# PSUM banks of an encoder layer's front shared out anew, and low-rank weights filled up to 128 rows

## The chip, the cores and the metric

The kernel runs on one core of one Trainium2 chip. TensorE (PE) multiplies 128-row tiles into PSUM, which has eight banks of 128 partitions x 512 float32; VectorE (DVE), ScalarE (ACT) and GpSimd (POOL) read the banks and compute elementwise; SyncE (SP) issues transfers, and ACT issues some as well. Each engine works through its own queue in order and waits on semaphores. The metric is the device time of one launch in microseconds, the median over runs.

## What is computed

One layer of an encoder on 256 tokens of width 1024: an input projection, two token mixers on its columns (a gated linear recurrence `hgrn2` with 8 heads of 128, and an RWKV-7 recurrence with 16 heads of 64, both in both directions), a gated merge of their outputs, a layer norm, and a mixture of 32 experts of which each token takes four. The part that the change touches is the RWKV branch's low-rank projections (`wl` and `a_lo` are 64 columns wide each):

```python
r, k, v, wl_f, wl_b, a_lo, g_lo = _split(p, RW_SPLITS)
decays = []
for d, wl in enumerate((wl_f, wl_b)):
    w = -jax.nn.softplus(-(w0[d] + jnp.tanh(wl) @ w_up[d])) - 0.5
    decays.append(jnp.exp(-jnp.exp(w)))
a = jax.nn.sigmoid(a0 + a_lo @ a_up)
g = jax.nn.sigmoid(g_lo) @ g_up
```

## The kernel before, in words

The **front** takes the tokens, transposes them (L188) and forms all products with the input weights. `dense_parts` (L129) is one dense product: it takes a PSUM bank `bank_d` (`bd`), loads two tiles of weights of 512 KB on SP's queue, and multiplies sixteen times (L154), 128 rows by 128 columns by 256 tokens. Readers on ACT, DVE or POOL then empty the bank. All small per-column parameters are loaded by fifteen transfers on ACT's queue into one tile `prm` (L182), which PE transposes once (L195) into a bank `bank_p`.

The RWKV branch works on four quarters `qi` of its columns (four heads each). For each, `rwkv_columns` makes the dense products, `rwkv_prepare` (L417) prepares the chunked form of the recurrence, and `rwkv_run` (L622) runs it, with banks `bank_c` (two) and `bank_y` (one). In `rwkv_prepare` the function `pair(r)`, called twice, multiplies the low-rank activations `lora` with `wup` (one product for each direction, L472) and with `aup` (L479), forms the bonus (L491, read by DVE at L492), and then the products of decayed keys (L546, 16 program matmuls for each direction, masked by DVE at L553). All of these take a bank `bank_p` (`bs`), of which there is one. `wup` holds the two directions one below the other, 64 rows each, so each product has a contraction of 64 rows. Then `inverse` inverts the 16 x 16 triangles on DVE by repeated steps (L581, L583) and joins them with small products (L598, L607), also in `bank_p`. `hgrn_mix` (L778) does the other mixer with one bank `bank_h`: DVE makes `KK` (L784), PE multiplies with it (L810, L811, then groups at L827, each copied out by DVE at L829), and the gate `og` reads a dense product's bank on ACT (L774) and DVE (L775).

The streams of work are generators that `interleave` (L377) merges by rates; the Tile scheduler then orders each engine's queue by a model of its own, in which the number of banks of each kind counts. So a change of the banks changes the order of many instructions. Once `rwkv_run` has finished, the **merge** follows (L1010 and on), and then the **experts**: their weights, 402 MB, stream through rings of SBUF tiles, and PE multiplies each as it lands (L1202, L1232). The order in that half is written out by hand.

The eight banks are shared out at L98.

Of the kernel before, what the change touches and what calls it, by code (L numbers as in the profile page):

```python
# [8 lines left out]
F32 = mybir.dt.float32  # L9
# [7 lines left out]
P = 128  # L17
S = 256
# [30 lines left out]
def tile_encoder(ctx: ExitStack, tc: tile.TileContext, A, out):  # L49
    nc = tc.nc  # L50
    V, SC, G, T = nc.vector, nc.scalar, nc.gpsimd, nc.tensor
# [40 lines left out]
    fc = front.enter_context(tc.tile_pool(name="fc", bufs=1))  # L92

    def bank(tag, bufs=None):
        return ps.tile([P, 512], F32, name="bank_" + tag, tag=tag, bufs=bufs)


    bd, bs, bc, bh, by = (lambda t=t, n=n: bank(t, n) for t, n in (("d", 3), ("p", 1), ("c", 2), ("h", 1), ("y", 1)))  # L98

    def cp(eng, out, in_):  # L100
        if eng is SC:
# [71 lines left out]
    n = 0  # L173
# [10 lines left out]
    for k in range(0, KT, 2):  # L184
        b = bd()
        for kk in range(2):
            for t in range(2):
                T.transpose(out=b[:, kk * 256 + t * P:kk * 256 + (t + 1) * P],  # L188
                            in_=x_tok[:, t, (k + kk) * P:(k + kk + 1) * P], identity=ident)
# [4 lines left out]
    b = bs()  # L194
# [123 lines left out]


    lora = fc.tile([P, 3, S], F32, name="lora")  # L320
    b = lora1
    shift(lora[:, 0, :], b[:, :S], "muw")
    shift(lora[:64, 1, :], b[:64, S:], "mua", n=64)
    SC.activation(lora[:, 0, :], lora[:, 0, :], AF.Tanh)
    b = lora2
# [91 lines left out]
    def rwkv_prepare(qi, rw, tmp):  # L417
# [6 lines left out]
        vt = rw.tile([P, 2, 2, P], F32, name="vt", bufs=2)  # L424
        box[f"prep{qi}"] = L, Y, vt, bon, BS, scl
        cq = slice(256 * qi, 256 * qi + 256)
        wup = tmp.tile([P, 256], F32, name="wup")
        nc.scalar.dma_start(out=wup, in_=A["rw_w_up"][0].rearrange("a l n -> (a l) n")[:, cq])
        aup = tmp.tile([64, 256], F32, name="aup")
        nc.scalar.dma_start(out=aup, in_=A["rw_a_up"][0][:, cq])  # L430
        KB = late.tile([P, 2, 2, S], F32, name="KB", tag="B")


# [6 lines left out]
        b = bs()  # L440
        for r in range(2):
            for t in range(2):
                T.matmul(b[:, 4 * r + 2 * t:4 * r + 2 * t + 2], lhsT=sq[:, r, t * P:(t + 1) * P],
                         rhs=blk[:, 0:P:64], start=True, stop=True)
        rs = rsqrt(tmp, b[:, :8], 8, 1.0, 1e-24, floor=True)
        yield 2
        b = bs()
        for r in range(2):
            for t in range(2):
                for h in range(2):  # L450
                    n = 4 * r + 2 * t + h
                    T.matmul(b[64 * h:64 * h + 64, r * S + t * P:r * S + (t + 1) * P],
                             lhsT=rs[:, n:n + 1].to_broadcast([P, 64]), rhs=ident, start=True, stop=True)
# [11 lines left out]
        def pair(r):  # L465
# [3 lines left out]
            sg = tmp.tile([P, 2, S], F32, name="sg", tag="sg")  # L469
            b = bs()  # L470
            for d in range(2):
                T.matmul(b[:, d * S:(d + 1) * S], lhsT=wup[64 * d:64 * d + 64, cj],  # L472
                         rhs=lora[64 * d:64 * d + 64, 0, :], start=True, stop=True)
                SC.activation(sg[:, d, :], b[:, d * S:(d + 1) * S], AF.Tanh, scale=0.5,
                              bias=col(hm, "w0", 8 * d + j))
            V.tensor_scalar(sg, sg, 0.5, 0.5, op0=OP.mult, op1=OP.add)
            at = tmp.tile([P, S], F32, name="at")
            b = bs()
            T.matmul(b[:, :S], lhsT=aup[:, cj], rhs=lora[:64, 1, :], start=True, stop=True)  # L479
            sigmoid(at, b[:, :S], col(hm, "a0", j))  # L480
            yield 1
            V.scalar_tensor_tensor(out=KBr[:, 1, :], in0=ASr[:, 0, :], scalar=-1.0, in1=at,
# [516 lines left out]
    b = by()  # L999
# [485 lines left out]
```

## Time and profile before

| what | value |
| --- | --- |
| time, median of 3 runs | 1590.78 us (1585.95 to 1590.83) |
| the profiled execution, its own time | 1591.12 us |
| span of the profiled execution | 1589.3 us |
| mean granted TensorE clock | 0.981 |
| PE busy | 1455.9 us (92%) |
| DVE busy | 591.2 us (37%) |
| ACT busy | 374.4 us (24%) |
| POOL busy | 95.0 us (6%) |
| read from HBM | 464.48 MB, 293 GB/s over the span |

The span runs from the first to the last instruction; the 1.8 us between it and the execution's time lie outside of what the engines do. The shares of busy time are means over stages with different limits, so they are read stage by stage.

### The profile page before, as it was taken

How to read it: one execution, taken by the hardware profiler on the slowest of the kernel's cores; microseconds unless marked ns; L12 is line 12 of the kernel's file. 1: busy time of each engine (PE TensorE's matmuls, PEld its weight loads, DVE VectorE, ACT ScalarE, POOL GpSimd, SP SyncE). 2: the span in 40 equal slices, each digit the busy share in tenths (PEclk: the TensorE clock that was granted, in tenths of full speed). 3: DMA queues.
4: the chain of work that ended last, by engine and by line, in shares of the span. 5: the costliest groups of instructions: out<-in, count | busy, mean ns of one | idle time of the engine just before them, and what ended most of it. 6: DMA issues, size and time to landing. Idle time of an engine off the chain costs nothing. (4 is left out here: it accounts for less than half of the span.)

```text
span 1589.3 us, 27117 instructions
## 1 busy us (share of the span) xinstructions
PE 1455.9 (92%) x11331; PEld 796.7 (50%) x11331; DVE 591.2 (37%) x1539; ACT 374.4 (24%) x983; POOL 95.0 (6%) x142
## 2 busy tenths in 40 slices
PE   8989989989988999999999999889999988988985
PEld 7667667667666897444444433244434323322321
DVE  4685885985983465112111111121112111111113
ACT  2426335335335243211111111101111100100100
POOL 0310210210210000000000000000000000000000
PEclk9999999999999999999999999989899999999998
DMA  6322322322344786799999999999999999999995
GB/s 190 108 69 68 86 72 67 86 74 70 99 140 134 262 311 241 305 419 415 418 417 416 417 418 416 417 418 416 416 418 418 415 418 417 416 417 418 416 419 208
DMA packets 133981, 467.36 MB, mean 294 GB/s; under 512 B 9544, under 2 KB 66780, under 8 KB 101084
## 3 DMA queue, kind: packets, MB, share of 16 engines
q1 hardware_dynamic: 129280, 460.88, 74.5%
q10 hardware_dynamic: 4572, 4.68, 0.9%
q8 instruction: 91, 1.49, 0.4%
q14 instruction: 38, 0.31, 0.1%
HBM read 464.48 MB, written 1.05 MB: 293 GB/s over the span
## 5 line engine op out<-in xcount | busy, mean ns | idle before, releaser
L154 PE MATMUL bank_d<-xT,wt 128*128 128x256 f32 x1200 | 311.5, 398 | 0.4 <-DMA wt<-in_w_in_dram 0.4
L154 PEld LDWEIGHTS bank_d<-xT,wt 128*128 128x128 f32 x1200 | 217.4, 193 | 39.8 <-issue 6.2
L1238 DVE SCALAR_TENSOR_TENSOR yl<-ypb,slotg,yh 128x512 fp32r<-128x512 f32 x32 | 24.0, 751 | 483.2 <-ACT yh L1237 460.1
L1202 PE MATMUL hpb<-ring_l,xg 128*64 128x512 f32 x416 | 98.7, 602 | 4.7 <-DMA ring_l<-in_moe_w_dram 4.7
L1202 PE MATMUL hpb<-ring_p,xg 128*64 128x512 f32 x416 | 98.5, 598 | 2.4 <-DMA ring_p<-in_moe_w_dram 2.4
L1184 DVE TENSOR_SCALAR ot<-tpb 128x256 fp32r<-128x256 f32 x32 | 13.6, 425 | 233.9 <-ACT tpb L1183 233.9
L1202 PE MATMUL hpb<-ring_r,xg 128*64 128x512 f32 x408 | 96.3, 598 | 4.4 <-DMA ring_r<-in_moe_w_dram 4.4
L1237 ACT ACTIVATE yh<-ypb,slotg 128x512 fp32r<-128x512 f32 x32 | 22.0, 689 | 309.1 <-PE ypb L1232 309.1
L1163 PE MATMUL tpb<-oh,x 128*128 128x256 f32 (+1 forms) x288 | 65.1, 369 | 4.2 <-ACT xg L1168 3.2
L1183 ACT ACTIVATE tpb<-tpb 128x256 f32<-128x256 f32 x32 | 11.8, 370 | 235.3 <-PE tpb L1181 232.1
L1163 PEld LDWEIGHTS tpb<-oh,x 128*128 128x128 f32 x288 | 48.0, 190 | 35.6 <-DVE glu L1214 17.9
L1149 POOL TENSOR_TENSOR ohg<-oh,gate 128x512 f32<-128x512 f32 (+1 forms) x9 | 8.6, 952 | 867.6 <-PE tpb L1181 849.8
L1202 PEld LDWEIGHTS hpb<-ring_l,xg 128*64 128x64 f32 x416 | 29.0, 138 | 56.7 <-issue 40.6
L1202 PEld LDWEIGHTS hpb<-ring_r,xg 128*64 128x64 f32 x408 | 28.1, 136 | 54.7 <-issue 40.2
L1202 PEld LDWEIGHTS hpb<-ring_p,xg 128*64 128x64 f32 x416 | 27.8, 136 | 51.8 <-issue 42.5
L1232 PE MATMUL ypb<-ring_l,aT 128*64 128x512 f32 x208 | 48.8, 597 | 5.0 <-DMA ring_l<-in_moe_w_dram 5.0
L1232 PE MATMUL ypb<-ring_r,aT 128*64 128x512 f32 x200 | 47.3, 598 | 6.4 <-DMA ring_r<-in_moe_w_dram 6.4
L1202 PE MATMUL hpb<-ring_q,xg 128*64 128x512 f32 x200 | 47.2, 597 | 4.5 <-DMA ring_q<-in_moe_w_dram 4.5
L1232 PE MATMUL ypb<-ring_p,aT 128*64 128x512 f32 x192 | 45.0, 599 | 6.9 <-DMA ring_p<-in_moe_w_dram 6.9
L1202 PE MATMUL hpb<-ring_s,xg 128*64 128x512 f32 x208 | 49.2, 598 | 2.2 <-DMA ring_s<-in_moe_w_dram 2.2
L1216 ACT ACTIVATE sgm<-glu 128x256 f32<-128x256 f32 x64 | 26.7, 418 | 102.6 <-DVE glu L1214 102.6
L1202 PE MATMUL hpb<-ring_e,xg 128*64 128x512 f32 x208 | 48.6, 598 | 1.5 <-DMA ring_e<-in_moe_w_dram 1.5
(332 smaller groups left out, 2214.5 us busy)
## 6 DMA issues: line engine op xcount, KB each, us to landing
ring_l<-in_moe_w_dram SPq DMA_DIRECT2D x78, 1024.0 KB
ring_p<-in_moe_w_dram SPq DMA_DIRECT2D x76, 1024.0 KB
ring_r<-in_moe_w_dram SPq DMA_DIRECT2D x76, 1024.0 KB
wt<-in_w_in_dram SPq DMA_DIRECT2D x84, 512.0 KB
ring_s<-in_moe_w_dram SPq DMA_DIRECT2D x40, 1024.0 KB
ring_e<-in_moe_w_dram SPq DMA_DIRECT2D x38, 1024.0 KB
ring_q<-in_moe_w_dram SPq DMA_DIRECT2D x38, 1024.0 KB
ring_b<-in_moe_w_dram SPq DMA_DIRECT2D x38, 1024.0 KB
```

The source lines that it names most:

```text
L154: T.matmul(o, lhsT=lhsT, rhs=rhs, start=n == 0, stop=n == last)
L1149: G.tensor_tensor(out=ohg[:, :, :n], in0=oh[:, :, :n], in1=gate[:, :, es[0]:es[0] + n].unsqueeze(3).to_broadcast([P, 2, n, 64]), op=OP.mult)
L1163: T.matmul(b[:, kk * 256:kk * 256 + ne * 64], lhsT=x1[t][:, n * P:(n + 1) * P], rhs=oh[:, t, :ne].rearrange("p e s -> p (e s)"), start=t = ...
L1183: SC.activation(b[:, :S], b[:, :S], AF.Copy, accum_out=sg)
L1184: V.tensor_scalar(ot, b[:, :S], 0.0, None, op0=OP.is_gt)
L1202: T.matmul(self.hbs[cc][64 * j:64 * j + 64, :], lhsT=self.xg[:, k, self.ei, :], rhs=self.w1[k][:, c0:c0 + 512], start=False, stop=k == KT - 1)
L1216: SC.activation(sgm[cc], glu[cc], AF.Sigmoid, scale=1.702)
L1232: T.matmul(yb[64 * j:64 * j + 64, :], lhsT=self.aT[:, k % 4, 64 * (k // 4):64 * (k // 4) + 64], rhs=self.w2[k][:, j * 512:(j + 1) * 512], ...
L1237: SC.activation(yh, yb, AF.Copy, scale=self.sg)
L1238: V.scalar_tensor_tensor(out=yl, in0=yb, scalar=self.sg, in1=yh.bitcast(F32), op0=OP.mult, op1=OP.subtract)
```

## The change

One bank goes from the dense products to the preparations: `bank_d` has two in place of three, `bank_p` two in place of one. And the low-rank weights get a tile `ups` that lives through the whole front and has 128 rows for each of three products, the half that doesn't belong to the product being zero: direction 0 in rows 0 to 63, direction 1 in rows 64 to 127, `a` in rows 0 to 63. The zeros are written once at the start, by DVE, and so is the unused half of `lora`'s second part. Every quarter loads its columns into the other halves with three transfers on ACT's queue in place of two. The three products then have a contraction of 128 rows.

```diff
--- before.py
+++ after.py
@@ -95,7 +95,7 @@
         return ps.tile([P, 512], F32, name="bank_" + tag, tag=tag, bufs=bufs)
 
 
-    bd, bs, bc, bh, by = (lambda t=t, n=n: bank(t, n) for t, n in (("d", 3), ("p", 1), ("c", 2), ("h", 1), ("y", 1)))
+    bd, bs, bc, bh, by = (lambda t=t, n=n: bank(t, n) for t, n in (("d", 2), ("p", 2), ("c", 2), ("h", 1), ("y", 1)))
 
     def cp(eng, out, in_):
         if eng is SC:
@@ -318,6 +318,10 @@
 
 
     lora = fc.tile([P, 3, S], F32, name="lora")
+    V.memset(lora[64:128, 1, :], 0.0)
+    ups = fc.tile([P, 3, 256], F32, name="ups")
+    V.memset(ups[64:128, 0:3:2, :], 0.0)
+    V.memset(ups[0:64, 1, :], 0.0)
     b = lora1
     shift(lora[:, 0, :], b[:, :S], "muw")
     shift(lora[:64, 1, :], b[:64, S:], "mua", n=64)
@@ -424,10 +428,9 @@
         vt = rw.tile([P, 2, 2, P], F32, name="vt", bufs=2)
         box[f"prep{qi}"] = L, Y, vt, bon, BS, scl
         cq = slice(256 * qi, 256 * qi + 256)
-        wup = tmp.tile([P, 256], F32, name="wup")
-        nc.scalar.dma_start(out=wup, in_=A["rw_w_up"][0].rearrange("a l n -> (a l) n")[:, cq])
-        aup = tmp.tile([64, 256], F32, name="aup")
-        nc.scalar.dma_start(out=aup, in_=A["rw_a_up"][0][:, cq])
+        for d in range(2):
+            nc.scalar.dma_start(out=ups[64 * d:64 * d + 64, d], in_=A["rw_w_up"][0][d][:, cq])
+        nc.scalar.dma_start(out=ups[0:64, 2], in_=A["rw_a_up"][0][:, cq])
         KB = late.tile([P, 2, 2, S], F32, name="KB", tag="B")
 
 
@@ -469,14 +472,13 @@
             sg = tmp.tile([P, 2, S], F32, name="sg", tag="sg")
             b = bs()
             for d in range(2):
-                T.matmul(b[:, d * S:(d + 1) * S], lhsT=wup[64 * d:64 * d + 64, cj],
-                         rhs=lora[64 * d:64 * d + 64, 0, :], start=True, stop=True)
+                T.matmul(b[:, d * S:(d + 1) * S], lhsT=ups[:, d, cj], rhs=lora[:, 0, :], start=True, stop=True)
                 SC.activation(sg[:, d, :], b[:, d * S:(d + 1) * S], AF.Tanh, scale=0.5,
                               bias=col(hm, "w0", 8 * d + j))
             V.tensor_scalar(sg, sg, 0.5, 0.5, op0=OP.mult, op1=OP.add)
             at = tmp.tile([P, S], F32, name="at")
             b = bs()
-            T.matmul(b[:, :S], lhsT=aup[:, cj], rhs=lora[:64, 1, :], start=True, stop=True)
+            T.matmul(b[:, :S], lhsT=ups[:, 2, cj], rhs=lora[:, 1, :], start=True, stop=True)
             sigmoid(at, b[:, :S], col(hm, "a0", j))
             yield 1
             V.scalar_tensor_tensor(out=KBr[:, 1, :], in0=ASr[:, 0, :], scalar=-1.0, in1=at,
```

Lines behind the change stand two or three higher in the kernel after (L472 becomes L475, L479 L481, L546 L548, L598 L600, L784 L786, L810 L812, L827 L829).

The order of PE's queue at its start, before: L188 transposes the input tokens, L195 the parameters, L154 is a dense product's matmul.

```order
L188 MATMUL bank_d<-ident,x_tok 128x128 x16
L154 MATMUL bank_d<-xT_75,wt 128x256 x24
L195 MATMUL bank_p<-ident,prm 128x116
L154 MATMUL bank_d<-xT_75,wt 128x256 x40
L443 MATMUL bank_p<-blk,sq 128x2 x4
```

The same place after the change:

```order
L188 MATMUL bank_d<-ident,x_tok 128x128 x12
L195 MATMUL bank_p<-ident,prm 128x116
L188 MATMUL bank_d<-ident,x_tok 128x128 x4
L154 MATMUL bank_d<-xT_75,wt 128x256 x64
L446 MATMUL bank_p<-blk,sq 128x2 x4
L154 MATMUL bank_d<-xT_75,wt 128x256 x5
```

L195 has moved ahead of all dense matmuls, and to before the last four transpositions of the input.

PE's queue in the second half of the pair stretch of the third quarter, before (L472 and L479 are the low-rank products, L491 the bonus, L546 the decay products, L737 and L741 belong to the end of the recurrence of the quarter ahead), up to the products with `KK` at L810:

```order
L154 MATMUL bank_d<-xT_75,wt 128x256 x10
L491 MATMUL bank_p<-sqb,blk 128x256
L154 MATMUL bank_d<-xT_75,wt 128x256 x3
L546 MATMUL bank_p<-L,BK 64x64 x16
L154 MATMUL bank_d<-xT_75,wt 128x256 x4
L546 MATMUL bank_p<-L,BK 64x64 x16
L154 MATMUL bank_d<-xT_75,wt 128x256 x2
L737 MATMUL bank_c<-ident,yn 128x128
L741 MATMUL bank_c<-lora,gup 128x256
L154 MATMUL bank_d<-wt,xT_75 128x256 x8
```

The same place after, where L812 is the first product with `KK`:

```order
L154 MATMUL bank_d<-xT_75,wt 128x256 x2
L646 MATMUL bank_y<-W,L 32x64 x4
L154 MATMUL bank_d<-xT_75,wt 128x256 x7
L493 MATMUL bank_p<-sqb,blk 128x256
L154 MATMUL bank_d<-xT_75,wt 128x256 x2
L548 MATMUL bank_p<-L,BK 64x64
L154 MATMUL bank_d<-xT_75,wt 128x256 x2
L548 MATMUL bank_p<-L,BK 64x64 x31
L646 MATMUL bank_y<-W,L 32x64 x4
L154 MATMUL bank_d<-xT_75,wt 128x256 x18
L154 MATMUL bank_d<-wt,xT_75 128x256 x9
L812 MATMUL bank_h<-hq,KK 32x32
```

Dense matmuls have left the places between the preparation's products, and 27 of them stand in one block behind the last of L548, directly ahead of L812.

DVE's queue around `KK` of that quarter, before (L581 and L583 are the steps of the inverse, L743 and L745 the recurrence's end):

```order
L581 TENSOR_TENSOR R<-N 128x44
L745 SCALAR_TENSOR_TENSOR obT<-bon,pv,bank_c 128x256
L583 TENSOR_TENSOR N<-N,R 128x11x4
L743 SCALAR_TENSOR_TENSOR bon<-bank_c,pv,bon 128x256
L581 TENSOR_TENSOR R<-N 128x50
L784 TENSOR_SCALAR KK<-FT 128x2x512
L583 TENSOR_TENSOR N<-N,R 128x10x5
L745 SCALAR_TENSOR_TENSOR obT<-bon,pv,bank_c 128x256
```

And after, where L583 and L585 are these steps and L87 belongs to the root for the norm of the recurrence's output:

```order
L583 TENSOR_TENSOR R<-N 128x44
L86 SCALAR_TENSOR_TENSOR nw_t<-nw_t,nw_y 128x8
L785 TENSOR_TENSOR QQ<-FT,hq 128x1024
L585 TENSOR_TENSOR N<-N,R 128x4x11
L87 SCALAR_TENSOR_TENSOR nw_y<-nw_t,nw_y 128x8
L786 TENSOR_SCALAR KK<-FT 128x2x512
L583 TENSOR_TENSOR R<-N 128x36
L733 TENSOR_SCALAR yn<-bank_y,gn_mv,nw_y 128x64
```

`KK` has moved from behind the fifth step of its kind (L581) to behind the eleventh (L583), with the norm's root and its statistics between.

## Rows read from the trace of the kernel before

**Rows 1.** The page, part 2: busy tenths in 40 slices of the span.
```profile
DMA  6322322322344786799999999999999999999995
```

**Rows 2.** Windows: length, busy PE PEld DVE ACT POOL, clock, DMA share, GB/s.
```profile
500.00:560.00 60.00, 60.00 (x511) 50.90 (x512) 21.76 (x70) 16.70 (x38) 0.29 (x1) 1.00 0.66 222
700.00:900.00 200.00, 198.89 (x1022) 81.06 (x1018) 32.78 (x78) 26.68 (x60) 2.10 (x2) 1.00 1.02 417
```

**Rows 3.** Windows of one middle quarter: pair stretch, rest, inverse stretch.
```profile
274.60:311.00 36.40, 33.91 (x340) 24.04 (x339) 30.79 (x79) 13.93 (x39) 10.97 (x12) 1.00 0.29 79
221.70:274.60 52.90, 51.35 (x899) 38.84 (x899) 32.12 (x99) 28.02 (x98) 5.76 (x11) 0.95 0.22 62
193.90:221.70 27.80, 22.15 (x270) 17.33 (x266) 27.18 (x69) 8.55 (x19) 2.99 (x4) 0.98 0.35 101
```

**Rows 4.** Windows: first quarter's three stretches; the last's inverse and rest.
```profile
45.20:82.50 37.30, 34.87 (x255) 25.96 (x254) 26.91 (x49) 17.67 (x47) 13.96 (x12) 1.00 0.37 104
82.50:112.80 30.30, 24.72 (x359) 19.00 (x355) 28.02 (x72) 9.13 (x30) 3.47 (x5) 0.94 0.30 87
112.80:157.60 44.80, 43.64 (x781) 32.68 (x781) 26.15 (x83) 24.02 (x78) 3.51 (x8) 0.96 0.22 61
426.20:460.20 34.00, 27.60 (x295) 21.39 (x294) 30.24 (x75) 12.22 (x24) 2.96 (x4) 0.90 0.52 167
460.20:549.50 89.30, 82.23 (x1119) 65.04 (x1119) 40.55 (x124) 33.98 (x103) 6.48 (x11) 1.00 0.50 163
```

**Rows 5.** Timeline of the start: start, us, engine, line, tile; SP, ACT, PE.
```profile
0.76 0.86 SPq L164 DMA_DIRECT2D x_tok<-in_x_dram  x2
9.74 0.28 ACTq L182 DMA_DIRECT2D prm<-in_ln_b_dram  x1
4.57 0.45 PE L188 MATMUL bank_d<-ident,x_tok 128*128 128x128 f32 x1 [4.57 <-DVE smask L218]
6.05 3.17 PE L188 MATMUL bank_d<-ident,x_tok 128*128 128x128 f32 x15 [1.04 <-DMA x_tok<-in_x_dram]
9.06 10.54 PE L154 MATMUL bank_d<-xT,wt 128*128 128x256 f32 x48
20.12 1.10 PE L154 MATMUL bank_d<-xT,wt 128*128 128x256 f32 x4 [0.42 <-DMA wt<-in_w_in_dram]
```

**Rows 6.** Timeline of PE beside a pair of the preparation.
```profile
293.88 0.70 PE L472 MATMUL bank_p<-lora,wup 64*128 64x256 f32 x2
295.57 0.70 PE L472 MATMUL bank_p<-lora,wup 64*128 64x256 f32 x2
309.85 1.15 PE L546 MATMUL bank_p<-L,BK 64*64 64x64 f32 x32 [1.62 <-DVE L L553]
313.13 3.62 PE L154 MATMUL bank_d<-wt,xT 128*128 128x256 f32 x16
```

**Rows 7.** Groups by form: count | busy, mean ns | idle before, who ended it.
```profile
L546 PE MATMUL bank_p<-L,BK 64*64 64x64 f32 x512 | 19.3, 221 | 8.7 <-DVE L L553 5.1 <-DVE bon L492 3.2 <-DVE L L533 0.3
```

**Rows 8.** Timeline: last readers of a dense bank (ACT, DVE).
```profile
334.43 0.60 ACT L774 ACTIVATE og<-bank_d 128x512 f32<-128x512 f32 x1
339.97 0.69 DVE L775 SCALAR_TENSOR_TENSOR og<-og,bank_d 128x512 f32<-128x512 f32 x1
```

**Rows 9.** PE idle at an inverse's end, the window behind it, a DVE copy.
```profile
221.21 0.50 PE L827 MATMUL bank_h<-QQ,KS 128*32 128x32 f32 x18 [3.35 <-DVE As L829]
220.40:227.20 6.80, 5.98 (x168) 4.35 (x168) 6.07 (x15) 1.41 (x4) 0.00 (x0) 0.50 0.01 2
337.77 0.27 DVE L829 COPY_PREDICATED As<-lmask,bank_h 128x128 f32<-128x128 int32 x1
```

**Rows 10.** Timeline of DVE: KK, an inverse step, and PE's wait for KK.
```profile
321.37 0.68 DVE L784 TENSOR_SCALAR KK<-FT 128x1024 f32<-128x1024 f32 x1
322.73 0.22 DVE L583 TENSOR_TENSOR N<-N,R 128x54 f32<-128x54 f32 x1
L810 PE MATMUL bank_h<-hq,KK 128*32 128x32 f32 x128 | 3.2, 203 | 0.6 <-DVE KK L784 0.6
```

## The prediction, made before the changed kernel had run

> **What bounds the kernel now.** I read the page's slices first. From the eighteenth slice (675 us) on the DMA digits are 9 [rows 1], and the windows say it exactly: between 700 and 900 us the DMA share is 1.02 at 417 GB/s [rows 2]. The experts' weights are streamed there, and no instruction of that half is changed. So the change can act only before it, and a front that ends later or earlier by some time moves the whole end by that time. Before 550 us the DMA engines are mostly free, and TensorE (PE) is what to look at: between 500 and 560 us it is busy for 60.00 of 60 us [rows 2]. The front repeats one pattern for each quarter of the heads, so I cut it into three stretches: **pair** (from the first `wup` product, L472, to the last decay product, L546), **inverse** (to L598) and **rest** (to the next pair). The windows of a middle quarter show two different limits [rows 3]. In the rest PE is busy for 51.35 of 52.90 us. In the inverse it is DVE, with 27.18 of 27.80. In the pair stretch it is 33.91 on PE and 30.79 on DVE of 36.40. First and last quarter look alike [rows 4]; the last pair repeats the middle one (36.4 us). So work that leaves PE in a pair stretch is worth something only down to DVE's own time, and a product that moves into a rest costs its full length there.
>
> **The unit of the sum.** Sixteen records of a dense product take 3.62 us [rows 6]. Each product of the program leaves two records, and the last record's own 0.38 us is not pace, so one costs (3.62 - 0.38)/15 x 2 = 0.432 us. Every change of places is counted in this.
>
> **1. Weights filled up to 128 rows.** From the start of one `wup` product to the next, with two dense products behind the first, 1.69 us pass [rows 6]. Six records at 0.216 us are 1.30, so a 64-row product costs 0.39 us more than one of 128 rows. There are 24 in the kernel (16 at L472, 8 at L479), so PE has up to 9.4 us less to do, 2.3 in each pair stretch. Some now stand beside other small products, where the array changes form anyway; the lower end is two thirds, 6 us. The Trainium skill (TensorEngine Tiling (Array Packing), Key Properties) says that a change of tiling mode drains TensorE; by that the saving is of this kind, and the trace agrees with 0.39 us for each. The same page (When to Use Tiling) speaks against the change: a contraction of at most 64 rows lets two products share the array, up to twice as fast. Here no two `wup` products stand side by side in the order of before, so that speed-up isn't taken and filling up loses none of it; had it been, eight pairs would cost 8 x 0.43 = 3.5 us more.
>
> **2. Three memsets and one more load per quarter.** The memsets run once, on DVE, while PE waits for the input until 6.05 us [rows 5], and nothing on PE needs the weights before the first pair at 45 us. The same bytes of `up` weights come in three loads for two, on ACT's queue, nearly a whole quarter before their use, since the tile is free after its last product in the pair stretch. Zero; without this cover, under 1 us.
>
> **3. Banks: three to two for dense products.** A bank is held from the start of its product (sixteen program matmuls, 16 x 0.432 = 6.9 us) to its last reader. The slowest readers I found are those of `og`: ACT starts at 334.43, when the product is done, and DVE ends at 340.66 [rows 8], 6.2 us. The next product but one cannot start before 6.9 us have passed. Two banks are therefore just enough: zero, at worst a wait of a microsecond in a few of the quarters.
>
> **4. Banks: one to two for the preparation.** This takes away waits of L546 for the bank's last reader (3.2 us for `bon`, and part of the 5.1 for L553 [rows 7]; the 1.62 us at 309.85 [rows 6] is one). But its main effect is on the order: the planner now needs fewer dense products to cover those waits, and the order listing shows them leaving the pair stretch for the rest. Counted there, a middle pair goes from 41 dense products to 27, the inverse from 37 to 36, the rest from 50 to 65; in the first quarter 53 to 33, 38 to 36, 36 to 58; in the last 16 leave the pair, 4 the inverse, and 20 come behind it.
>
> *Pair.* PE would need 33.91 - 14 x 0.432 - 2.3 = 25.5 us, DVE's 30.79 stay. With the 0.6 us that the DVE-bound inverse loses beyond DVE's busy time I take 31.4, **-5.0**. First quarter: 26.91 + 0.6 = 27.5, **-9.8**. *Inverse.* Four copies of `bank_h` at 0.27 us [rows 9] stand behind it now: **-1.1**. *Rest.* Middle: 15 x 0.432 = 6.5; two `bank_h` groups that come with them, 0.5 each [rows 9], 1.0; together +7.5. From this goes a gain: its first 5.5 us run at a clock of 0.50 [rows 9], after PE sat idle for 3.35 us on a `bank_h` result that is now used elsewhere. Half clock for 5.5 us is 2.7 us of work; I credit half, 1.4, as the idle may come back in another place: **+6.1**. So a middle quarter comes to -5.0 - 1.1 + 6.1 = 0.0, twice. First: 22 x 0.432 = 9.5, +1.0 - 1.4 = +9.1; with -9.8 and -1.1 it is **-1.8**. Last: -5.0 - 1.1; behind it 20 x 0.432 = 8.6 and 1.0 more, against 7.1 us in which PE waits in the first recurrence steps (82.23 of 89.30 [rows 4]). In the order of after some 16 products stand there, which fill these waits; I take 5.5 of them: +4.1, in all **-2.0**.
>
> **5. The start.** The order moves `prm`'s transposition (L195) from behind 24 dense products to a place ahead of all, behind twelve of the sixteen input transpositions. It needs all fifteen parameter loads; the last is issued at 9.74 us on ACT's queue [rows 5]. Before, dense products started at 9.06, and L195 came only when the first 48 records ended, at 19.60, without a wait for `prm`. How long such a load is on its way no row shows. The input, issued at 0.76, let PE begin at 4.57 and go on at 6.05 [rows 5], so 3.8 to 5.3 us for far more bytes; below, a small load could take some 2 us, an estimate. I take 3.8, so L195 starts at 13.5; it and four transpositions of 0.21 us last 1.1. Dense products start at 14.6 for 9.06, 5.5 later, less the old pause around L195 (20.12 - 19.60 = 0.5): **+5.0**, between +3.2 and +6.5. PE is the limit behind it, so nothing hides this.
>
> **Sum:** +5.0 - 1.8 + 0.0 - 2.0 = +1.2 on the profiled execution's 1591.1 us. The median of the runs lies 0.3 lower, so **1592**. The uncertain terms (start 3.2 to 6.5, filled waits 0 to 7, the clock's credit 0 to 2.7 in three quarters, 6 to 9.4 for the forms) reach 6 to both sides.
>
> **The rivals.** *A, faster.* DVE isn't the floor that I set: the scheduler's second bank lets preparation overlap the neighbouring stretches, and PE's saved work shows in full. Then 1591.1 + 5.0 - 9.4 - 3.2 (the `bon` waits) = 1583.5, by the median **1583**. For it: in both PE-bound windows every us of PE is time. Against: 30.79 us of DVE in a stretch of 36.40. The Trainium skill (Perfetto Trace Analysis, Consistent bubbles) says that a gap which repeats on the engine to be saturated can mean too few buffers; the waits at L546 (8.7 us) are such a gap, though the row names another engine than a bank for 5.1 of them.
>
> *B, slower.* One mechanism, at the first `bank_h` products. Behind the last decay product a block of 27 dense products (11.7 us) stands now, and next to it products that need `KK`. On DVE `KK` comes ahead of the twelfth step of the inverse instead of the sixth. Before, it was done 11 us after the last decay product (321.37 + 0.68 against 311.0 [rows 6, 10]), and PE waited 0.6 us in all for it [rows 10]. Six steps of two operations at 0.22 us put it 2.6 us later, the statistics between them perhaps two more. PE would then idle for 2 to 4 us, and behind idle of this length the clock stood at 1.2 GHz for 6.8 us [rows 9], half of 2.4, a loss of 3.4 us. An inverse of 26.7 us with 21.7 of PE hides 5.0 us of idle and lost clock; beyond an idle of 1.6 us it shows. At 3.9 it is 2.3 us in each of four quarters: **1601**. For it: the order. Against: before loses as much at the inverse's end, and that wait goes.
>
> *C, the change doesn't do what it says.* The forms cost nothing less, since the array changes form beside them anyway; the start's loss stands alone: 1591.1 + 5.0 - 0.3 = **1595.8**.
>
> **How the numbers follow.** About 0.3% (4.8 us) is what can be told from no change: below 1586.0 is faster, above 1595.6 slower. My forecast gets 0.44, nearly all of it within these bounds (0.02 on either side). A gets 0.29, B 0.23, C 0.04, which lies on the edge. Faster: 0.29 + 0.02 = 0.31; slower: 0.23 + 0.02 + 0.02 = 0.27; no change: 0.42. The range takes in A's centre and B's, 1581 to 1602, and leaves out the parts of A and B beyond (0.1 each); my forecast alone would be 1586 to 1598.
>
> **What would show it.** Dense products start near 14.6 us, with PE idle behind twelve transpositions. L475 and L481 take no longer than a dense product. The pair stretch of a middle quarter is 31 us long with DVE busy all through, the rest 59. PE before 550 us has no new wait for a dense bank. B shows as idle in front of L812 with a releaser `KK` and a clock of 0.50 behind it. I am wrong if the pair stretch falls well under 30 us (A), if dense products start before 12 us, or if the slices behind 675 us don't shift with the front.

## The result

The changed kernel takes **1567.38 us** (median of 4 runs, 1564.13 to 1570.5), the one before 1590.8: a ratio of 0.9857, 95% interval 0.9825 to 0.9889. It is faster by 23 us, where the prediction said no change (1592, range 1581 to 1602). The profiled execution, the fastest of the four, takes 1564.13 us, span 1562.3.

The windows of the changed kernel, each pair cut at its first `wup` product as in [rows 3]; first the pair, inverse and rest of a middle quarter, then those of the first quarter, then the last quarter's three, then a stretch of the experts. (The first pair of [rows 4] starts at 45.20, 2.4 us ahead of its first `wup` product at 47.57; cut there it takes 35.0 us.)

```profile
158.86:187.58 28.72, 27.76 (x341) 20.57 (x341) 25.91 (x53) 10.65 (x28) 9.71 (x9) 1.00 0.25 75
187.58:209.55 21.97, 19.23 (x182) 15.48 (x182) 21.76 (x83) 8.88 (x23) 1.47 (x4) 1.00 0.37 100
209.55:267.53 57.98, 55.37 (x984) 43.23 (x984) 37.53 (x112) 31.22 (x106) 8.26 (x15) 1.00 0.29 80
51.38:80.56 29.18, 24.97 (x215) 19.72 (x214) 24.41 (x46) 15.55 (x44) 10.80 (x12) 1.00 0.33 96
80.56:104.97 24.41, 20.25 (x216) 16.45 (x215) 22.86 (x53) 4.51 (x8) 0.52 (x1) 0.93 0.36 103
104.97:158.86 53.89, 51.74 (x921) 40.94 (x922) 32.09 (x101) 29.01 (x100) 7.11 (x13) 0.94 0.24 67
376.25:404.97 28.72, 27.75 (x341) 20.58 (x341) 25.91 (x53) 10.61 (x28) 9.70 (x9) 1.00 0.23 67
404.97:429.29 24.32, 20.78 (x190) 16.82 (x190) 23.71 (x85) 11.29 (x26) 1.47 (x4) 1.00 0.51 141
429.29:523.57 94.28, 91.78 (x1258) 73.30 (x1258) 49.20 (x143) 38.61 (x115) 9.30 (x16) 1.00 0.56 187
700.00:900.00 200.00, 199.96 (x1025) 81.07 (x1024) 32.34 (x76) 27.12 (x61) 2.10 (x2) 1.00 1.02 417
```

A middle quarter, put together from these stretches, falls from 117.1 us to 108.7: the pair from 36.4 to 28.7, the inverse from 27.8 to 22.0, and the rest grows from 52.9 to 58.0. DVE is busy for 5 us less in each of the first two stretches, and for 5 us more in the rest, where PE is the limit and DVE has room. The experts stream at the same 417 GB/s as in [rows 2], so the front's earlier end moves the end of the kernel. That the front ends earlier is seen at the router's first product, which stands behind all of it, before

```profile
548.90 1.87 PE L1001 MATMUL bank_y<-rwt,gb 128*128 128x32 f32 x16
```

and in the changed kernel

```profile
523.57 1.87 PE L1003 MATMUL bank_y<-rwt,gb 128*128 128x32 f32 x16
```

It is 25.3 us, and the spans of the two executions differ by 27.0. Cut at each quarter's first `wup` product, these 25.3 us are +3.8 at the start, -2.5 in the first quarter, -8.3 and -6.5 in the middle two and -11.8 in the last, where the forecast had +5.0, -1.8, 0.0, 0.0 and -2.0. Behind the router's product, where no instruction was changed, the executions profiled for this document take between 1036 and 1044 us, so what a single front gains shows in the time only to within some 4 us.

The start in the changed kernel, which answers to [rows 5]: PE waits behind twelve transpositions until L195 can run, and dense products begin at 14.52 us.

```profile
5.98 2.80 PE L188 MATMUL bank_d<-ident,x_tok 128*128 128x128 f32 x11 [0.97 <-DMA x_tok<-in_x_dram]
13.44 0.43 PE L195 MATMUL bank_p<-ident,prm 116*128 116x116 f32 x1 [4.66 <-DMA ups<-in_rw_w_up_dram]
14.52 1.92 PE L154 MATMUL bank_d<-xT,wt 128*128 128x256 f32 x4
```

**A ledger of the front.** The front is cut into thirteen windows, the start and three for each quarter, from 0 to the router's first product. For each of them, PE's idle time is the length less PE's busy time, and the work lost to the clock is the length times (1 - granted clock). What is left is PE's work at full clock. Summed, in us:

| kernel | router at | PE idle | lost to the clock | PE work at full clock |
| --- | --- | --- | --- | --- |
| before | 548.9 | 50.2 | 11.7 | 487.0 |
| changed | 523.6 | 40.8 | 4.9 | 477.9 |
| e1 banks only | 532.5 | 41.7 | 10.7 | 480.2 |
| e2 padding only | 549.7 | 54.5 | 17.7 | 477.5 |
| e3 padding, two and one | 549.4 | 56.6 | 10.1 | 482.6 |
| e9 = e7, L195 later | 518.9 | 34.3 | 6.8 | 477.8 |
| e10 = e7, 64 rows | 531.5 | 39.3 | 13.1 | 479.1 |
| e11 own bank for L548 | 541.4 | 50.0 | 13.4 | 478.0 |

So the 25.3 us are 9.4 of idle and 15.9 of PE's busy time, which the table parts into 6.8 of clock and 9.1 of work. This last parting is rough: PE's idle time at half clock counts in both columns, so the work comes out too small where much is lost to the clock. e2 and e3 have the same products, and their last column differs by 5.1 us.

What the padding takes from PE's work is read better in the four pair stretches, which hold all 24 low-rank products and, in these four kernels, ran at a clock of 1.00. PE's busy time in them falls by 6.8 us from the kernel before to e2 (from 33.91 to 32.24 in a middle one) and by 2.0 us from e1 to the changed kernel (28.03 to 27.76). It is less with the new banks in part because some of the 64-row products stand side by side in that order: in e1, in the second half of each pair stretch, the second `wup` product and the `aup` product start together, at 175.07 us in the second quarter, and the next matmul starts 0.63 us later, where the padded two take 0.96 us (175.54 to 176.50). The prediction looked for such neighbours only in the order of before, which has none.

So the prediction had the work and part of the clock, and almost nothing of the idle. The waits of PE by group show where it went. Before (L827 is the `bank_h` group that [rows 9] has one instance of; L546 and L810 stand in [rows 7] and [rows 10]):

```profile
L827 PE MATMUL bank_h<-QQ,KS 128*32 128x32 f32 x640 | 10.9, 209 | 17.1 <-DVE As L829 6.7 <-DVE N L583 5.2 <-ACT KS L102 3.8
```

and in the changed kernel, the same three groups (L829, L548, L812):

```profile
L829 PE MATMUL bank_h<-QQ,KS 128*32 128x32 f32 x640 | 9.9, 203 | 4.6 <-ACT KS L102 1.7 <-DVE QQ L879 1.6 <-POOL QQ L879 0.7
L548 PE MATMUL bank_p<-L,BK 64*64 64x64 f32 x512 | 20.6, 222 | 5.5 <-DVE L L535 3.8 <-POOL L L535 1.6
L812 PE MATMUL bank_h<-hq,KK 128*32 128x32 f32 x128 | 3.7, 214 | 7.9 <-DVE KK L786 7.9
```

L827's 17.1 us are 4.6 now, L546's 8.7 are 5.5, and L810's 0.6 are 7.9: -12.5, -3.2 and +7.3. None of the rows names `bon` or the mask L553 any more; what the decay products wait for now is their own input (L535, the operands that DVE and POOL form), and not a bank.

### The profile page after: what moved, and what is told of

It reads as the page before. It is cut to its first block, busy times and chain, and to the rows that moved or that the text cites. A ratio compares the mean times of both kernels' runs of the same rounds, so it can differ in the third digit from the quotient of the medians.

```text
span 1562.3 us, 27109 instructions
## 1 busy us (share of the span) xinstructions
PE 1438.9 (92%) x11331; PEld 797.1 (51%) x11331; DVE 578.5 (37%) x1542; ACT 374.0 (24%) x983; POOL 91.6 (6%) x142
## 5 line engine op out<-in xcount | busy, mean ns | idle before, releaser
L154 PE MATMUL bank_d<-xT,wt 128*128 128x256 f32 x1200 | 298.3, 391 | 0.3 <-DMA wt<-in_w_in_dram 0.3
L154 PEld LDWEIGHTS bank_d<-xT,wt 128*128 128x128 f32 x1200 | 218.9, 192 | 34.2 <-issue 1.3
L1185 ACT ACTIVATE tpb<-tpb 128x256 f32<-128x256 f32 x32 | 11.8, 368 | 235.6 <-PE tpb L1183 232.3
L1218 ACT ACTIVATE sgm<-glu 128x256 f32<-128x256 f32 x64 | 26.7, 417 | 102.7 <-DVE glu L1216 102.7
```

The source lines that it names most:

```text
L154: T.matmul(o, lhsT=lhsT, rhs=rhs, start=n == 0, stop=n == last)
L1185: SC.activation(b[:, :S], b[:, :S], AF.Copy, accum_out=sg)
L1218: SC.activation(sgm[cc], glu[cc], AF.Sigmoid, scale=1.702)
```

## The experiments

Each run's median is over 4 to 12 executions, beside 11 to 23 of the kernel before on the same chip; the chips differ between the groups below, so runs of two groups are compared by their ratios. PE's queue stands in the same order in the kernel before and in e2, and in the changed kernel and e1. So the banks alone set PE's order, and the padding changes no place in it.

**e1, e2, e3, e4.** e1 takes the kernel before with the new line for the banks; e2 the changed kernel with the old one; e3 the changed kernel with `("d", 2), ("p", 1)`; e4 adds to the changed kernel one constraint:

```diff
-    T.transpose(out=b[:, :nrow], in_=prm[:nrow, :], identity=ident[:nrow, :nrow])
+    with tc.issue_after(lastmm[0].ins):
+        T.transpose(out=b[:, :nrow], in_=prm[:nrow, :], identity=ident[:nrow, :nrow])
```

> The two-and-two banks with the low-rank weights as before, 64 rows each. Built, the queues stand in the order of the changed kernel. Theory: the gain of about 23 us is made of 9.4 us from the 24 products of 128 rows, about 7 us less of half-clock stretches, and about 9 us less idle of PE (the late start already taken off); the last two come from the banks, through the order. So this kernel should be near 1591 - 14 = 1576 (1573 to 1580), with pair stretches of about 31 us, and the 64-row products still 0.39 us dearer each. Rival: the padding is what shortens the pair stretch, and the banks only move work from there to the rest; then it is 1588 to 1596, and the late start shows as a loss.

> 128-row weights with the banks of before (three and one); the queues of PE stand in the order of before. Theory: PE loses 0.39 us at each of 24 products, 9.4 us in all, and half to all of it shows: 1581 to 1586. Rival: DVE and the single bank hold the pair stretch, so the saved time becomes idle of PE in front of L548: 1588 to 1592, with more idle there than the 8.7 us of before.

> 128-row weights, two banks for dense products, one for preparations (one bank unused). PE's queue is in the order of before except for the parameters' transposition, which stands at the start as in the changed kernel. Theory: the third dense bank was never needed, so this is the kernel with the banks three and one plus the late start, about 5 us slower than that one: 1586 to 1592. Rival: two banks make dense products wait for their readers, and it is 8 us or more slower than that one, with idle in front of L154 named for a reader of a dense bank.

> The changed kernel with one constraint on the order: the parameters' transposition is issued behind the first 24 dense matmuls, as in the kernel before; all else on PE stands as it did. Theory: the late start (dense products at 14.5 us in place of 9.1) costs 4.5 to 5.5 us of the whole, so this is 1562 to 1563, about 5 us under the changed kernel. Rival: the time lost at the start is hidden later (by loads or DVE), and it stays within 1 us of the changed kernel's 1567.

| run | median us | ratio to before, interval |
| --- | --- | --- |
| e1 banks only | 1570.38 | 0.9874 (0.9854 to 0.9894) |
| e2 padding only | 1587.49 | 0.9981 (0.9966 to 0.9995) |
| e3 padding, two and one | 1592.86 | 1.001 (0.9994 to 1.0026) |
| e4 late parameters | 1571.28 | 0.9878 (0.9853 to 0.9902) |

e1 gains 20 us, more than its theory gave it: the banks carry nearly all of the change. Its ratio, 0.9874, is that of the changed kernel's second run (e8, 0.9873), and 0.0017 above that of the first; beside the new banks the padding is worth 0 to 3 us, which isn't told from nothing. Middle quarter of e1, pair, inverse, rest:

```profile
157.82:187.22 29.40, 28.03 (x340) 20.13 (x341) 25.86 (x53) 10.62 (x28) 9.71 (x9) 1.00 0.24 71
187.22:209.68 22.46, 20.49 (x183) 16.47 (x183) 21.99 (x83) 8.84 (x23) 1.48 (x4) 0.92 0.33 94
209.68:269.32 59.64, 57.07 (x985) 44.03 (x984) 37.57 (x113) 31.21 (x106) 8.24 (x15) 0.97 0.29 79
```

The pair is 0.7 us longer than in the changed kernel, where the prediction had 2.3 for the six 64-row products; in this order each of the six has another small product on one side, or one of the six; in the order of before three of six have.

e2 is the surprise of the four. PE is busy for 6.8 us less in its pair stretches, within the forecast's 6 to 9.4, and only 3 us come out. Pair, inverse and rest of a middle quarter, and two groups of waits:

```profile
272.86:308.15 35.29, 32.24 (x340) 24.42 (x338) 30.82 (x79) 13.95 (x39) 10.82 (x12) 1.00 0.29 81
308.15:335.81 27.66, 22.06 (x267) 17.27 (x267) 27.04 (x69) 8.53 (x19) 3.01 (x4) 0.98 0.36 101
335.81:387.67 51.86, 51.14 (x899) 38.96 (x899) 32.08 (x99) 27.79 (x98) 5.75 (x11) 0.94 0.22 63
```

```profile
L548 PE MATMUL bank_p<-L,BK 64*64 64x64 f32 x512 | 19.3, 221 | 8.6 <-DVE L L555 5.1 <-DVE bon L494 3.2
L829 PE MATMUL bank_h<-QQ,KS 128*32 128x32 f32 x640 | 10.9, 208 | 19.6 <-DVE As L831 6.7 <-ACT KS L102 5.4 <-DVE N L585 5.3
```

The pair is 1.1 us shorter than before, not 2.3. PE's idle in it grows from 2.5 to 3.1 us; the waits at L548 are those of [rows 7], and those of the `bank_h` groups grow from 17.1 to 19.6. So of the 6.8 us, 2.9 became idle within the pair stretches, and these are 3.9 us shorter in all. The theory of half to all of 9.4 us fell; the rival had the size, but put the idle in front of L548, where it didn't grow. The profiled execution lost more to the clock than that of before (17.7 us for 11.7); the ratio of the medians says 3 us.

e3 is 5.4 us slower than e2, about its late start, by which its first pair begins 5.3 us later (53.56 for 48.28). L154 waits for 0.3 us in all for a load, and for 0.2 to 0.5 us in three groups for their operands, and no wait of L154 names a reader of a bank. So no cost of two dense banks is seen once the kernel runs. e4 says where the third one was used. Its dense products start at 9.8 us, and then wait:

```profile
21.47 0.26 PE L198 MATMUL bank_p<-ident,prm 116*128 116x116 f32 x1
25.08 5.19 PE L156 MATMUL bank_d<-xT,wt 128*128 128x256 f32 x15 [3.35 <-ACT sh_t L311]
```

The two banks hold the low-rank inputs until L311 on ACT reads them, which needs the parameters; so the third product waits 3.35 us, half clock follows (0.84 on the mean of the next 11 us), and nothing is gained. The theory of e4 was wrong on the remedy; its price is what e7 tests next.

**e7, e8, e9: the transposition behind twelve matmuls.** The first dense product is run in two parts, with L195 between them:

```diff
-    lora1 = dense(w_in, C_LORA, X)
-    lora2 = dense(w_in, C_LORA + 64, X, tiles=(1,))
+    first = dense_parts(w_in, C_LORA, X)
+    for _ in range(3):
+        next(first)
...
+    lora1 = run_all(first)
+    lora2 = dense(w_in, C_LORA + 64, X, tiles=(1,))
```

> The changed kernel, with the parameters' transposition behind twelve dense matmuls: late enough for its loads (landed by 13.4 us in the changed kernel's trace), early enough that the two dense banks come free in time (run e4 waited 3.35 us for one, and ran at half clock behind it). Theory: the start costs 5 us, so this kernel is 4 to 5 us under the changed kernel beside it: 1562 to 1564. Rival: the first stretch isn't what sets the end, and it is within 1.5 us of it.

> The changed kernel again, on the same chip as the three beside it, to compare with. 1565 to 1570; first pair at 51.4 us, middle pair stretches 28.7 us, inverses 22.0, rests 58.0. If the half-clock stretches are what spreads single runs, its executions differ by up to 6 us while these stretches at full clock stay equal.

> Run e7 again (the changed kernel with the parameters' transposition behind twelve dense matmuls), to compare the three beside it with on the same chip: 1560 to 1565.

e7 takes 1564.25 us, the changed kernel beside it (e8) 1569.99; the ratios to before are 0.9819 (0.9799 to 0.984) and 0.9873 (0.9851 to 0.9896). e9 repeats 0.9821. The late start costs the changed kernel 5.7 us by the medians, and the forecast had 5.0. e7 is faster than both kernels. Its start:

```profile
9.87 6.62 PE L156 MATMUL bank_d<-xT,wt 128*128 128x256 f32 x24
16.32 0.27 PE L199 MATMUL bank_p<-ident,prm 116*128 116x116 f32 x1
16.43 5.35 PE L156 MATMUL bank_d<-xT,wt 128*128 128x256 f32 x24
```

**e5, e6: the other mixer's place, and three banks for dense products.**

```diff
-            yield ("at", c * QUARTER + 50)
+            yield ("at", c * QUARTER + 75)
```

> 128-row weights, the banks of before (three and one), and the other mixer's stream set 25 units later in the table that merges the streams, so that its bank_h groups stand behind the inverse on PE and DVE, as they do in the changed kernel. Theory: most of the gain is this order (the groups no longer sit inside the inverse, with the 3.3 us idle of PE and the half clock behind it), and a second bank isn't needed for it: inverse stretches fall from 27.7 to about 23 us, and the time from 1587.5 to 1570-1578. Rival: the second bank itself gives the gain (its pair stretches stay at 35 us here and the work only moves to the rest): 1584 to 1590.

> The changed kernel, but with three banks for dense products, two for preparations and one for the RWKV recurrence in place of two, two and two. Theory: two banks for preparations and the old start (dense products near 9 us) together would give about 1562, if the recurrence could do with one bank; its products L687, L698, L712 wait for the readers of the bank before, so pay 0.3 to 0.7 us in many of 28 steps: 1565 to 1580. Rival: the third dense bank gains what the recurrence loses, and it is under 1565.

e5 has the padding, the banks of before and the other mixer 25 units later. It takes 1588.59 us (0.9978, 0.9966 to 0.999): its theory falls in the time. A middle quarter, pair, inverse, rest, and the wait of the `bank_h` groups:

```profile
272.65:307.92 35.27, 32.69 (x340) 24.53 (x338) 30.82 (x79) 13.59 (x37) 10.27 (x12) 1.00 0.30 81
307.92:330.48 22.56, 18.71 (x150) 15.23 (x149) 21.67 (x62) 6.93 (x20) 1.09 (x2) 1.00 0.45 123
330.48:385.73 55.25, 52.08 (x1016) 39.80 (x1017) 38.10 (x106) 30.06 (x100) 7.19 (x13) 1.00 0.21 59
```

```profile
L829 PE MATMUL bank_h<-QQ,KS 128*32 128x32 f32 x640 | 10.9, 210 | 16.2 <-ACT KS L102 15.0 <-issue 0.9 <-DVE QQ L879 0.2
PE bank_h L829 <- ACT KS L102: 15.0, 6, 11.2
```

(The last line is of the view of waits: us in all, times, longest.)

The inverse does fall, to 22.6 us from e2's 27.7, and DVE's load with it; but the rest grows to 55.3 from 51.9, and the pair stays at 35.3. Less DVE work in the inverse is worth 0.5 and 1.7 us of the two middle quarters, for 7.3 and 6.1 between e2's and the changed kernel's. The last quarter is no test of the order: 11.2 us of the 16.2 are one wait in it, for an ACT copy (KS) that stands behind ACT's wait for a load of the experts' biases (more below). Without that wait e5 might come into its theory's range; no run shows it. The pair gets short only where the preparation has two banks: e6 (`("d", 3), ("p", 2), ("c", 1)`) has middle pairs of 30.7 us. Its dense products start at 9.2 us, and yet it takes 1590.07 us (0.9981, 0.9962 to 1.0), so its theory and its rival both fall: the last stretch takes 113.6 us with 14.2 of PE idle. The recurrence has one bank there, but the longest waits in that stretch name no reader of it (4.9 us at L860 and 2.8 at L609 name none at all, 2.7 at L656 is for a copy on ACT), so that the one bank is the cause isn't shown.

**e10, e11, e12: single parts of e7.** e10 reads 64 rows of the same tiles. e11 gives the decay products a bank of their own, `("p", 1), ("k", 1)`. e12 exchanges the two instructions that form `QQ` and `KK`.

> Run e7 with the low-rank products back at 64 rows (the same tiles and loads, only the rows read); every queue stands in the same order. Theory: each of the 24 products costs PE up to 0.39 us more, but with two banks two of the three stand beside other small forms, where the array changes form anyway, so only 3 to 5 us of 9.4 show: 3 to 5 us slower than e7. Rival: all of it shows, now that PE bounds every stretch: 9 us slower.

> Run e7 with the second preparation bank given to the decay products (L548) alone, the other one to all else of the preparation (low-rank products, bonus, inverse). The waits for the bonus reader go, those of the second decay product for the mask of the first stay. Theory: the gain comes from any product taking whichever bank is free, above all the second decay product while DVE masks the first; so the pair stretch goes back most of the way, from 28.7 to 32 us or more, and the time to 1572-1580. Rival: separating the bonus and low-rank products from the decay products is what counts: pair stretch under 30 us and within 3 us of e7.

> Run e7 with KK formed before QQ on DVE (two instructions of the other mixer exchanged), since PE waits 1.8 us for KK behind its block of dense products in each quarter, and QQ (1.2 us) stands before it. Theory: this wait shrinks to about 0.7 us and the half clock behind it (clock 0.92 in the inverse stretches) goes: 2 to 6 us faster than e7. Rival: PE's idle there only moves behind the bank_h products, and it is within 1.5 us of e7.

| run | median us | ratio to before, interval |
| --- | --- | --- |
| e9 | 1561.2 | 0.9821 (0.9799 to 0.9843) |
| e10 64 rows | 1566.63 | 0.9844 (0.9824 to 0.9864) |
| e11 own bank | 1583.88 | 0.9964 (0.9948 to 0.998) |
| e12 `KK` first | 1568.11 | 0.9856 (0.9836 to 0.9877) |

e10's interval overlaps e9's; the medians lie 5.4 us apart, the ratios 3.7 us, so a gain of the padding isn't told from nothing here either. In e11 the theory of the pair fell (30.1 us, not 32): freeing the low-rank and bonus products from the decay products brings most of the shorter pair. But the rival, which had the time within 3 us of e7, fell as well. Of the 22.5 us by which e11's front ends later than e9's, 11.0 lie in the last stretch, 106.5 us for e9's 95.5. e12 missed both its theory and its rival: it isn't faster than e9 but some 6 us slower by the ratios (the intervals just overlap), and PE waits for `KK` no less than without the exchange, 8.1 us in all for e9's 7.4. The profiled execution of e12 is its slowest; of the 11.6 us by which its front ends later than e9's, 7.8 lie in the last stretch. Last stretch and its longest wait, of e9, e11 and e12:

```profile
423.42:518.88 95.46, 91.85 (x1258) 73.23 (x1258) 48.96 (x143) 38.62 (x115) 9.21 (x16) 1.00 0.55 184
```

```profile
470.01 0.43 PE L704 MATMUL bank_c<-gs,Y 32*32 32x64 f32 x16 [1.23 <-ACT Z L102]
```

```profile
434.87:541.37 106.50, 95.52 (x1249) 75.62 (x1249) 49.29 (x142) 37.85 (x111) 8.30 (x14) 0.92 0.50 165
```

```profile
487.41 0.66 PE L693 MATMUL bank_c<-W,L 128*32 128x64 f32 x16 [6.17 <-ACT W L102]
```

```profile
427.21:530.51 103.30, 95.31 (x1222) 75.88 (x1222) 47.27 (x141) 38.05 (x114) 8.81 (x16) 0.93 0.51 170
```

```profile
479.56 0.65 PE L704 MATMUL bank_c<-gs,Y 32*32 32x64 f32 x16 [4.04 <-DVE gs L104]
```

In e11 and e12 one wait of 4 to 6 us for ACT or DVE, and half clock behind it. ACT's waits ahead of it in e11 name a load (columns: us in all, times, longest):

```profile
ACT bias L297 <- DMA BK<-in_moe_b_dram: 7.6, 1, 7.6
```

The experts' biases are loaded and split on ACT in four parts, and what stands behind a split in ACT's queue waits for the load too. Summed from 380 to 549 us, before and changed:

```profile
ACT bias L291 <- DMA BK<-in_moe_b_dram: 23.2, 4, 8.0
```

```profile
ACT bias L291 <- DMA BK<-in_moe_b_dram: 8.4, 4, 5.4
```

Before, e2, e3, e5 and e6 have 23 to 25 us here, those with two and two shared banks 8 to 13, e11 19.6. In the kernel before this wait reaches PE: a split waits 7.84 us for its load, the copy `KS` stands behind it, and PE idles for that copy.

```profile
449.25 0.84 ACT L291 ACTIVATE bias<-BK 128x768 bf16<-128x768 f32 x1 [7.84 <-DMA BK<-in_moe_b_dram]
450.00 0.61 ACT L102 ACTIVATE KS<-KK 128x512 f32<-128x512 f32 x1
450.67 0.66 PE L827 MATMUL bank_h<-QQ,KS 128*32 128x32 f32 x32 [3.84 <-ACT KS L102]
```

So 3.8 of the 17.1 us at L827 are the biases', and another 2.0 us at 480.70, for a copy behind the next split. The changed kernel's loads are not much quicker; there ACT has copies of the recurrence to do between the issue and the split. Third load before (issued by 472.47) and changed (by 449.32):

```profile
479.14 0.84 ACT L291 ACTIVATE bias<-BK 128x768 bf16<-128x768 f32 x1 [8.00 <-DMA BK<-in_moe_b_dram]
454.74 0.84 ACT L291 ACTIVATE bias<-BK 128x768 bf16<-128x768 f32 x1 [0.73 <-DMA BK<-in_moe_b_dram]
```

The split starts 6.7 us behind the issue before and 5.4 in the changed kernel, but ACT waits for 8.0 and 0.7 us. What these waits are worth two runs try.

**e13, e14: the biases loaded quarter by quarter.**

```diff
             yield from rwkv_prepare(c, rw, tmp)
+            split_biases(tmp, c)
...
             yield from gate_part(C_GA + 256 * n, [tmp.tile([P, 512], F32, name="gate", tag=t_)])
-            split_biases(tmp, n)
```

> The kernel before, with one move: the experts' biases, a quarter of them at a time, are loaded and split behind each quarter's preparation, and no longer all in the last stretch, where ACT waited 23.2 us in all for their loads (the expert weights stream at the same time) and recurrence steps queued behind it. Theory: the last quarter's idle and half clock in the kernel before (its three stretches take 159.1 us, for 147.3 in the changed kernel) are mostly this wait, so they fall to 148-152 us and the time by 7 to 11 us, to 1580-1584. Rival: these waits are beside other work and the order of the banks sets the last quarter; then it stays within 3 us of 1591.

> The same move in the kernel of run e7. There ACT waited only 8.8 to 10.8 us for these loads, mostly beside other work. Theory: under 4 us to gain, 1558 to 1562, with fewer executions in which the last stretch is long. Rival: nothing to gain, or a loss of a few us, since the earlier loads put their splitting on ACT and DVE into stretches that DVE bounds: 1562 to 1570.

Last quarter of e13 (banks of before), pair, inverse, rest, and an earlier inverse:

```profile
396.87:433.24 36.37, 33.90 (x340) 24.03 (x339) 30.77 (x79) 12.71 (x35) 10.97 (x12) 1.00 0.26 74
433.24:462.00 28.76, 23.62 (x257) 18.35 (x257) 26.82 (x70) 10.65 (x24) 3.45 (x4) 1.00 0.55 183
462.00:546.21 84.21, 82.45 (x1151) 65.44 (x1152) 35.57 (x122) 31.15 (x100) 5.75 (x11) 1.00 0.50 161
313.72:347.19 33.47, 26.42 (x256) 20.38 (x256) 26.71 (x70) 10.65 (x24) 2.68 (x4) 0.90 0.36 95
```

The last quarter falls from 159.1 to 149.3 us, as the theory said, with the banks of before. But it isn't the wait alone that left: three of the four splits did too, and DVE is busy for 62.4 us in its inverse and rest, for 70.8 in [rows 4]. And ACT now waits for these loads in the earlier quarters as well (18.9 us in all four), an earlier inverse is 33.5 us in place of 27.7, and the whole gains 3 us: 1587.4 (0.9982, 0.9969 to 0.9995). So the theory held for the quarter and the rival for the time. In e14 there is nothing to gain: 1564.7 (0.9841, 0.9821 to 0.9862), although ACT waits 24.6 us there for the loads. A sum of ACT's waits is no price: a wait counts only where PE stands behind it.

## Why the prediction was wrong

1. *128 rows: right as work in the old order, too large as time.* PE is busy for 6.8 us less in the pair stretches (e2), 0.28 us a product where the forecast took up to 0.39. Alone it gives 3 us, as PE then waits for DVE and `bank_h`. With the new banks, the case that was forecast, it is 2.0 us of work, in part because four pairs of 64-row products run side by side there when they aren't padded, and 0 to 4 us of time (e1, e10), not told from nothing.
2. *Memsets and loads: right.* No wait names them in the pair stretches. At the start a row names an `ups` load for L195's wait; L195 reads only the parameters, whose last load stands in the same queue ahead of it. In e1, which has no more loads than before, L195 starts as late (13.39 us for 13.44).
3. *Three to two dense banks: right in the pattern* (e3), but at the start the third bank had covered the wait for the parameters (e4), which the forecast's 6.9 us rule for a bank didn't see.
4. *The second preparation bank: the step that failed.* I kept each stretch's DVE work where it was ("DVE's 30.79 stay", and 1.1 us out of the inverse), and so put the pair at 31.4, the inverse at 26.7. They are 28.7 and 22.0, as DVE work leaves both (30.8 to 25.9 and 27.2 to 21.8 us) for the rest. By the rule of the sum a middle quarter was to stay equal, and the two lost 8.3 and 6.5 us. The order of DVE was there to be read; I counted four copies out of it. But less DVE work is only part of it: in e5 it leaves the inverse without a second bank, which shortens the inverse as much (22.6 us) and a middle quarter by 0.5 to 1.7 us only. The account on PE is: in the first of the two its idle falls from 9.7 to 6.3 us, its work by 1.7, and the half clock in it (3.2 us) goes; in the other they are 9.1 to 6.2, 2.1 and 1.5. I had no term for the 17.1 us that PE waits at L827, though one of its rows stood in [rows 9]. The first pair was moreover cut 2.4 us ahead of its first `wup` product; cut there, the rule gives -9.0 for the forecast's -9.8.
5. *The last quarter: -2.0 was -11.8.* I let 5.5 us of its idle be filled. What I missed is ACT's wait for the bias loads, 23.2 us before and 8.4 after, behind which PE idled for 5.8 us, and the clock fell to 0.70 on the mean of 450 to 460 us. e13 takes 9.8 us out of the last quarter by moving loads and splits together, and loses most of it elsewhere, so how much of the 11.8 us is this wait stays open. I had not looked at what ACT waits for there.
6. *The start: right, in part by luck.* 14.52 us for 14.6, and 5.7 us by e7 for 5.0. The last parameter load was issued at 9.19 us and not at 9.74, and L195 came 4.25 us behind it and not 3.8; the two errors cancel.

*Rival A* had the right sign and half of the reason, and its sign, a pair well under 30 us, came true: preparation does overlap the neighbouring stretches with the second bank, and DVE's 30.8 us were no floor. The other half, PE's saved work showing in full, is not what happened (3 us of 6.8 in e2, 0 to 4 us with the new banks). Of its 8 us the waits at L546 did fall by the 3.2 us that it counted; it left out the 12.5 us at L827 and the clock. *Rival B* saw the place: PE waits for `KK` now, 7.9 us in all, behind a block of 27 dense products. The price was wrong. In the execution profiled first the clock stood at 1.00 behind that wait in three quarters of four:

```profile
201.60 0.28 PE L812 MATMUL bank_h<-hq,KK 128*32 128x32 f32 x7 [1.82 <-DVE KK L786]
```

In e8, the same kernel again, and in e7 it fell in the middle quarters behind a wait as long, and the inverse was only 0.4 us longer (22.36 and 22.34 us, clock 0.92), with DVE busy for 22.0 of it. The rule of the Trainium skill on the drain at a change of tiling mode (TensorEngine Tiling (Array Packing), Key Properties) agrees with e2: 24 products without the change of form are 6.8 us less of PE's busy time. The rule of the Trainium skill on small contractions (the same page, When to Use Tiling) had nothing to lose in the order of before, as the forecast said; in the new order e1 bears it out, 0.63 us for two 64-row products side by side and 0.96 for the padded two.

What stays open: the number of banks sets the scheduler's order too, and no run here holds the order and changes the bank alone. Shown is that the second bank, with the order it brings, gives 20 us (e1), and that the order's most visible part, the other mixer behind the inverse, gives a middle quarter little without it (e5 beside e2). What it would give in the last quarter without ACT's wait for the biases wasn't tried.

## What to carry to other kernels

Count the two engines of an interleaved stage together: a freed bank lets the scheduler move work of the second engine as well, so the limit of a stretch isn't fixed by what stands in it now. Sum all waits of the limiting engine by group before pricing a change, and look at what the late queues wait for. A saving on the busy engine is worth only what doesn't turn into idle: 6.8 us of work alone were 3 us of time. And judge a change of single products in the order that the kernel will have, not in that of before.

## What was not expected of the hardware

The same program loses a different amount to the clock from one execution to the next, and at other places: e7 and e9 are the same kernel, run on two chips, and the last stretch of e9 (above) took 95.46 us at a clock of 1.00, that of e7

```profile
423.78:522.59 98.81, 93.42 (x1258) 74.23 (x1257) 49.20 (x143) 38.61 (x115) 9.60 (x16) 0.98 0.55 179
```

An idle of 3.35 us was followed by 1.2 GHz for 6.8 us in the kernel before [rows 9], one of 4.66 us at the start of the changed kernel was not. A single profile's half-clock stretches are therefore no stable term of a sum; by the ledger's rule the runs here lose 2 to 19 us of a front of 519 to 550 to them.
